# Recurrence preparation traced ahead, fewer vector operations in the projection stage, and a new order of the modulation, in a two-layer diffusion backbone on one core

## The chip, the cores and the metric

The kernel runs on one core of one Trainium2 chip. The core has engines that run side by side, each taking its own instructions in order: TensorE (PE in the profile, with its weight loads as PEld), VectorE (DVE), ScalarE (ACT), GpSimd (POOL) and SyncE (SP), which here only issues DMAs. ACT and POOL issue some DMAs too. Engines wait for each other through semaphores. The metric is the device time of one execution in microseconds (us). Lower is better.

## The reference

Two layers work on 512 latent tokens of width 1024 and, in the first layer, on 256 context tokens with their own conditioning vector. Each sub-layer is norm, modulation, mixer, norm, gate, residual:

```python
def modulate(h, shift, scale):
    return h * (1 + scale) + shift
def ada_mod(cvec, w, b):
    m = jax.nn.silu(cvec) @ w + b          # six vectors of width 1024
...
        ml = ada_mod(c, ada_w[layer], ada_b[layer])
        mc = ada_mod(c_ctx, ada_w[layer], ada_b[layer])
        hl = modulate(rmsnorm(xl, norm_mix_pre[layer]), ml[0], ml[1])
        if layer % 2 == 0:
            yc, yl = mixer_ab(hc, hl, ...)
        else:
            yc, yl = mixer_mlstm(hc, hl, ...)
        xl = xl + ml[2] * rmsnorm(yl, norm_mix_post[layer])
        hl = modulate(rmsnorm(xl, norm_ffn_pre[layer]), ml[3], ml[4])
        xl = xl + ml[5] * rmsnorm(conv_ffn(hl, ...), norm_ffn_post[layer])
```

The mixer of the first layer projects its input to 23 blocks of 128 columns. Eight of them feed a gating part, which for each of 4 groups and each chunk of 128 tokens norms `v`, multiplies it by a 128x128 matrix over the tokens and gates it with `u`. The other 15 feed a recurrence that runs over the tokens in both directions with 8 heads:

```python
    def step(s, inp):
        r_t, w_t, k_t, v_t, kk_t, b_t = inp
        sa = jnp.einsum('bhvk,bhk->bhv', s, kk_t)
        s = s * w_t[:, :, None, :] - sa[..., None] * b_t[:, :, None, :] + v_t[..., None] * k_t[:, :, None, :]
        return s, jnp.einsum('bhvk,bhk->bhv', s, r_t)
```

## The kernel before

Everything is float32. A projection is split in a high and a low part and made of three matmul passes (lines 266 to 268). The first layer's mixer has three stages.

**Lead-in.** The six token tiles are loaded on ACT's queue, normed and transposed (L363) to `xT`, one 128-column tile `kt` of 8 at a time. Meanwhile `ada_gen(0, ...)` (L144) makes shift and scale of the first modulation: 16 loads of 512 KB on SP's queue, row block by row block of `ada_w`, each multiplied by `silu` (L157) into one bank that sums over the row blocks. So no column of the modulation is there before the last row block. Only then `scale_vec` and L374 to L376 make the modulated halves `hT`, and the first two units (named lora) are projected, first all latent, then all context columns.

**Projection stage.** A *unit* is one block of 128 output columns: `load_w` loads 512 KB, ACT makes the high part (L124), POOL the low part (L125), and PE makes 24 latent matmuls (`pl_`) and 24 context matmuls (`pc_`). `kr(ct)` makes the units of k and r for channel tile `ct` (0 to 3, two heads each), `v(ct)` that of v. `sgu(g)` is the gating part of group `g`: two units (`u`, `vg`), then per group of 2 or 4 token tiles transposes (`vt`), a square sum on ACT (L782), two POOL operations for the inverse root (`rstd_from`, L228 and L229), a scaling on DVE (L784), and a matmul (`pz`, L788), tile by tile.

The preparation of the recurrence has three parts for each `ct`. `prep_e` makes decays and keys (matmuls kkn, zw, za, bon, the rest on DVE and ACT). `prep_n` multiplies them in 24 chunks of 64 tokens (`nx`, `ny`, L532 and L533) and copies blocks of the result to `NF` (L538 to L541, on ACT for nx, on DVE for most of ny). `prep_t` inverts 24 triangular matrices a side: DVE transposes `NF` to `Ai` (L552) and `On` (L554), then a recurrence of 31 steps follows, two DVE operations each (L566, L568), which builds `Ti`. Two transposes (`Td` L573, `Tn` L574), copies to `TT` on ACT (L580, L581), and two groups of small matmuls (`w` L588, copied to `Wm` by L591, then `t` L597, copied to `TT` by L600) end it. NF, On and Ti have one buffer each; Ai, Td and Wm share one.

Loops are written as Python generators. `weave` (L302) interleaves several of them in proportion to given lengths, which gives the order in which instructions are traced. A planner then places each instruction: per engine it takes, among those that it believes ready by its own estimates, the one traced earliest. `tc.high_priority(offset=n)` lowers the rank of what is traced inside it by n, as if it had been traced n instructions earlier. Once placed, each engine keeps its order. After `kr(0)`, `prep_e(0)` is woven with `v(0)` and `kr(1)`; then for ct = 0, 1, 2 `prep_t(ct)` is woven with `prep_e(ct+1)` and `prep_n(ct+1)`, and with `v(ct+1)`, `kr(ct+2)` and `NA[ct]` of the 16 parts of the gating.

**Chain stage.** The pools of the stage before are closed, and the recurrence runs over 12 chunks for the pairs of channel tiles (0, 1) and (2, 3), in six blocks `b` of `chains` (L923 on): three per pair. Each block is woven with the loads and matmuls for the next (`preps`), with `prep_t(3)` in block 0 (`inverse`), and with the next two parts of the modulation (`ada_gen(1)`, `ada_gen(2)`, one yield per row block) in blocks 1 and 2. After block 2 `run(ada)` makes their tail, and `gate_rows` and `scale_vec` use them. `finish` of the first pair (means, variances, gate) runs in blocks 3 and 4 with a single PSUM bank, "7".

The output projection, the first feed-forward part and the second layer follow. PSUM has 8 banks, "0" to "7"; `bank(name, role)` takes the banks in the string `role` in turn.

Of the kernel before, what the change touches and what calls it, by code (L numbers as in the profile page):

```python
# [8 lines left out]
F32 = mybir.dt.float32  # L9
F32R = mybir.dt.float32r  # L10
AF = mybir.ActivationFunctionType
ALU = mybir.AluOpType
# [4 lines left out]
KT = 8  # L17
# [57 lines left out]
def _build(ctx, tc, xall, par, cst, ada_w, ada_t, w_in, w_out, ffn_up, ffn_down, lora, wsT, a_bs, c_in, c_gate, c_out, mneg, parf, parm, out):  # L75
# [68 lines left out]
    def ada_gen(g, pool, tag, rawb, cols=1024, rtag="araw", width=None):  # L144
# [5 lines left out]
        for kt in range(KT):  # L150
            for c0 in range(0, n, cols):
                pl = pool[(c0 // cols) % len(pool)] if isinstance(pool, list) else pool
                raw = pl.tile([P, width], F32, tag=rtag, name=f"ada{g}{kt}{c0}", bufs=rawb)[:, :cols]
                nc.sync.dma_start(raw, ada_w[kt, :, g * 2048 + c0:g * 2048 + c0 + cols])
# [175 lines left out]
    with ExitStack() as lx:  # L330
# [10 lines left out]
        with ExitStack() as nx:  # L341
            npool = nx.enter_context(tc.tile_pool(name="nrm0", bufs=1))
            xt = [npool.tile([P, D], F32, tag="xt", name=f"x0_{i}", bufs=6) for i in range(6)]
            for i in (2, 3, 4, 5, 0, 1):
                nc.scalar.dma_start(xt[i], xall[i])
            ag = ada_gen(0, npool, "67", 6)
            silu_rows("67")
            for _ in range(KT):
                next(ag)
            xT = npool.tile([P, KT, T], F32, name="xT0")  # L350
            for (t0, nt, c0) in ((2, 4, 0), (0, 2, TL)):
                dgs = []
# [6 lines left out]
                w = nt * 128  # L359
                for kt in range(KT):  # L360
                    pt = bank(f"nT_00{t0}{kt}", "243501")
                    for i in range(nt):
                        nc.tensor.transpose(pt[:, i * 128:(i + 1) * 128], xt[t0 + i][:, kt * 128:(kt + 1) * 128], ident)  # L363
                    (A.copy if kt % 2 else V.tensor_copy)(xT[:, kt, c0:c0 + w], pt[:, :w])
            run(ag)
            scale_vec(0, 0)
            lw01 = [load_w(w_in[20 + i], f"win{20 + i}") for i in range(2)]
            lps = [[], []]
            for (cnd, c0, w) in ((0, 0, TL), (1, TL, TC)):
                hh, hl = hT[2 * cnd:2 * cnd + 2]  # L370
                for kt in range(KT):
# [5 lines left out]
                for i in range(2):  # L377
                    lps[i].append(proj_pass(lw01[i], hT, f"lora{i}", "0167", cnd))
# [142 lines left out]
        def prep_n(ct):  # L521
# [6 lines left out]
            for g8 in range(3):  # L528
# [6 lines left out]
                for (pp, b0, e) in ((px, 0, A), (py, 64, V)):  # L535
# [11 lines left out]
        def prep_t(ct, prbank):  # L547
# [5 lines left out]
            On = wkT.tile([P, 24, 32], F32, tag="On", name=f"On{ct}")  # L553
            V.transpose(On, NF[:, 1, 0:24])  # L554
# [3 lines left out]
            for s_ in range(31):  # L558
# [199 lines left out]
        def sgu(g):  # L758
# [13 lines left out]
            for (t0, nt) in ((0, 2), (2, 4)):  # L772
# [4 lines left out]
                vns = []  # L777
                for i in range(nt):
                    tk = t0 + i
                    ss = sm.tile([P, 1], F32, tag="ss", name=f"sgss{g}{tk}", bufs=6)  # L780
                    vn = wkR.tile([P, P], F32, tag="vn", name=f"vn{g}{tk}", bufs=5)
                    A.activation(vn, pt[:, i * 128:i * 128 + 128], AF.Square, accum_out=ss)  # L782
                    r = rstd_from(ss, f"sg{g}{tk}", 1.0 / 128)
                    V.tensor_scalar(vn, pt[:, i * 128:i * 128 + 128], r, None, ALU.mult)  # L784
                    vns.append(vn)
                pz = bank(f"pz{g}{t0}", role)
                for i in range(nt):
                    mm(pz[:, i * 128:i * 128 + 128], vns[i], wsT_s[:, g * 128:g * 128 + 128], start=True, stop=True)  # L788
# [138 lines left out]
        for b, (k, g) in enumerate(blocks):  # L927
# [24 lines left out]
            if b == 4:  # L952
# [601 lines left out]
```

## Time and profile before

| | us |
|---|---|
| median of 3 runs | 1988.01 (1987.05 to 1990.56) |
| profiled execution | 1996.04 |
| its span, first to last instruction | 1994.3 |
| PE / DVE / ACT / POOL busy in the span | 1862.3 / 1343.8 / 782.6 / 319.4 |

The page cuts the span in 40 slices of 50 us; each digit is the busy share in tenths. Here are the three rows that matter:

```profile
PE   6998988589997999999999999999999989999998
DVE  3498766783345479999995336676777677777533
...
PEclk8999789698998999999999999999999989999999
```

PEclk is the TensorE clock that was granted. The mixer of the first layer fills the first 13 slices. A group of instructions is named by its line, engine, operation and tiles (written `<-` read); "idle before" is how long the engine stood before them, and what ended that.

### The profile page before, as it was taken

The page shows a single profiled execution, that of the slowest core. Times are in us where ns is not written, and L with a number is a line of the kernel's source. Part 1 is how long each engine was busy: PE and PEld are TensorE (multiplying, and loading weights), DVE is VectorE, ACT ScalarE, POOL GpSimd, SP SyncE. Part 2 cuts the span into 40 slices and gives each one's busy share as a digit, 9 for nine tenths or more (in the row PEclk, how much of TensorE's full clock was granted, in tenths as well). Part 3 has the DMA queues.
Part 4 walks back from the last instruction along what each step waited for, and adds up shares of the span by engine and source line. Part 5 has one row for each costly group of instructions (what it writes and reads, how often), then busy time and mean ns, then how long its engine had stood idle before and what let it go on. Part 6 is the DMA issues. An engine that isn't in the chain of part 4 may idle for free.

```text
span 1994.3 us, 31593 instructions
## 1 busy us (share of the span) xinstructions
PE 1862.3 (93%) x12307; PEld 1502.4 (75%) x12307; DVE 1343.8 (67%) x2635; ACT 782.6 (39%) x1382; POOL 319.4 (16%) x459
## 2 busy tenths in 40 slices
PE   6998988589997999999999999999999989999998
PEld 2876666476675878888888887778888768888886
DVE  3498766783345479999995336676777677777533
ACT  4455545332244442222222225575544343333322
POOL 2222233220100222223221002000110020000001
PEclk8999789698998999999999999999999989999999
DMA  7132121356643424444441324421111312222222
GB/s 289 64 130 104 65 105 43 118 158 197 187 113 138 160 89 157 144 167 167 152 146 62 106 95 150 167 82 42 44 43 43 127 66 95 95 94 90 92 95 85
DMA packets 102694, 227.76 MB, mean 114 GB/s; under 512 B 28160, under 2 KB 42704, under 8 KB 100496
## 3 DMA queue, kind: packets, MB, share of 16 engines
q1 hardware_dynamic: 100192, 219.90, 32.3%
q10 hardware_dynamic: 2192, 5.04, 0.7%
q8 instruction: 97, 1.59, 0.3%
q0 software_dynamic: 160, 0.79, 0.1%
q14 instruction: 53, 0.43, 0.1%
HBM read 199.31 MB, written 26.39 MB: 113 GB/s over the span
## 4 chain that ended last, share of the span: by engine, by line
PE 58%; DVE 2%; ACT 1%; POOL 1%; issue 1%; DMA 0%; DVEq 0%; SPq 0%; POOLq 0%; ACTq 0%
PE of L992 5%; PE of L993 5%; PE of L991 5%; PE pl_fb L268 4%; PE pl_fb L267 4%; PE pl_fa L268 4%; PE pl_fb L266 4%; PE pl_fa L267 4%; PE pl_fa L266 4%; PE pd L1399 1%; PE pe L1376 1%; PE pc_fb L266 1%; PE pc_fa L266 1%; PE pc_fa L267 1%; PE pc_fb L267 1%; PE pc_fb L268 1%
## 5 line engine op out<-in xcount | busy, mean ns | idle before, releaser
L1039 DVE SCALAR_TENSOR_TENSOR cv<-pl_fa,fpar,cv 128x441 f32<-128x441 f32 (+2 forms) x352 | 243.2, 691 | 18.5 <-ACT cv L1028 13.1
L993 PE MATMUL of<-hi_fd,hlo 128*128 128x512 f32 x440 | 173.7, 397 | 3.0 <-DVE hlo L1063 3.0
L992 PE MATMUL of<-lo_fd,hhi 128*128 128x512 f32 x440 | 174.3, 396 | 1.5 <-DVE lo_fd L125 1.5
L991 PE MATMUL of<-hi_fd,hhi 128*128 128x512 f32 x440 | 173.4, 396 | 0.0
L201 DVE SCALAR_TENSOR_TENSOR aj<-am,srb 128x512 f32<-128x512 f32 x224 | 163.7, 731 | 4.8 <-DMA am<-in_ada_t_dram 0.3
L1063 DVE TENSOR_TENSOR hlo<-hid,hhi 128x512 fp32r<-128x512 f32 (+1 forms) x66 | 39.2, 601 | 133.6 <-ACT hhi L1062 133.4
L1062 ACT ACTIVATE hhi<-hid 128x512 fp32r<-128x512 f32 (+1 forms) x66 | 36.7, 558 | 176.4 <-PE of L992 173.0
L993 PEld LDWEIGHTS of<-hi_fd,hlo 128*128 128x128 f32 x440 | 83.4, 190 | 22.5 <-DVE hlo L1063 3.4
L992 PEld LDWEIGHTS of<-lo_fd,hhi 128*128 128x128 f32 x440 | 83.0, 189 | 21.8 <-DVE lo_fd L125 2.7
L222 POOL TENSOR_SCALAR rstd_p_f<-sq_f,sq_f 128x1 f32<-128x1 f32 x10 | 6.8, 680 | 570.3 <-ACT jk_f L970 570.3
L991 PEld LDWEIGHTS of<-hi_fd,hhi 128*128 128x128 f32 x440 | 83.1, 189 | 19.8 <-ACT hi_fd L124 0.4
L125 DVE TENSOR_TENSOR lo_fd<-raw_fd,hi_fd 128x1024 fp32r<-128x1024 f32 x66 | 80.8, 1224 | 25.1 <-ACT hi_fd L124 24.9
L124 ACT ACTIVATE hi_fa<-raw_fa 128x1024 fp32r<-128x1024 f32 x44 | 46.5, 1058 | 92.6 <-PE pl_fb L267 66.7
L124 ACT ACTIVATE hi_fd<-raw_fd 128x1024 fp32r<-128x1024 f32 x66 | 69.2, 1049 | 27.8 <-DMA raw_fd<-in_ffn_down_dram 11.1
L124 ACT ACTIVATE hi_fb<-raw_fb 128x1024 fp32r<-128x1024 f32 x44 | 46.7, 1061 | 74.4 <-PE pc_fa L267 42.9
L125 POOL TENSOR_TENSOR lo_win<-raw_win,hi_win 128x1024 fp32r<-128x1024 f32 x23 | 56.9, 2476 | 92.9 <-ACT hi_win L124 92.8
L268 PE MATMUL pl_fa<-h0f_lathi,lo_fa 128*128 128x512 f32 x176 | 70.3, 399 | 0.0
L268 PE MATMUL pl_fb<-h0f_lathi,lo_fb 128*128 128x512 f32 x176 | 70.3, 399 | 0.0
L268 PE MATMUL pl_fb<-h1f_lathi,lo_fb 128*128 128x512 f32 x176 | 70.2, 399 | 0.0
L268 PE MATMUL pl_fa<-h1f_lathi,lo_fa 128*128 128x512 f32 x176 | 70.2, 399 | 0.0
L1041 ACT ACTIVATE cv<-cv 128x512 f32<-128x512 f32 x44 | 27.8, 632 | 106.4 <-DVE cv L1039 106.4
L125 POOL TENSOR_TENSOR lo_fb<-raw_fb,hi_fb 128x1024 fp32r<-128x1024 f32 x22 | 59.0, 2684 | 65.0 <-ACT hi_fb L124 65.0
(631 smaller groups left out, 5520.2 us busy)
## 6 DMA issues: line engine op xcount, KB each, us to landing
raw_fd<-in_ffn_down_dram SPq DMA_DIRECT2D x66, 512.0 KB, 3.2
am<-in_ada_t_dram SPq DMA_DIRECT2D x112, 256.0 KB, 2.9
raw_fa<-in_ffn_up_dram SPq DMA_DIRECT2D x44, 512.0 KB, 3.3
raw_fb<-in_ffn_up_dram SPq DMA_DIRECT2D x44, 512.0 KB, 3.2
ada<-in_ada_w_dram SPq DMA_DIRECT2D x24, 512.0 KB, 6.4
raw_win<-in_w_in_dram SPq DMA_DIRECT2D x23, 512.0 KB, 3.2
ada<-in_ada_w_dram SPq DMA_DIRECT2D x8, 1024.0 KB, 5.3
raw_cin<-in_c_in_dram SPq DMA_DIRECT2D x16, 512.0 KB, 3.5
```

Source lines behind the costliest of these rows:

```text
L124: nc.scalar.activation(hi[:, c], raw[:, c], AF.Copy)
L125: strm.sub.tensor_tensor(lo[:, c], raw[:, c], hi[:, c].bitcast(F32), ALU.subtract)
L201: V.scalar_tensor_tensor(place(f"aj{i}{h}{cnd}", "junk"), raw, 1.0, sb[cnd * 2 + h], ALU.mult, ALU.mult, accum_out=acc[:, cnd, h:h + 1])
L266: mm(p, wh[:, kt, :], hh[:, kt], start=(kt == 0), stop=False)
L267: mm(p, wh[:, kt, :], hl[:, kt], start=False, stop=False)
L268: mm(p, wl[:, kt, :], hh[:, kt], start=False, stop=(kt == KT - 1))
L991: mm(o[i][hf], hi, w[0][:, c], start=f, stop=False)
L992: mm(o[i][hf], hi, w[1][:, c], start=False, stop=False)
L993: mm(o[i][hf], lo, w[0][:, c], start=False, stop=e)
L1039: V.scalar_tensor_tensor(dv, src[:, r0 + dy:r1 + dy, c0 + dx:c1 + dx], fw(ky * 3 + kx), dv, ALU.mult, ALU.add)
L1062: A.activation(hi, hid[cnd][:, k], AF.Copy)
L1063: V.tensor_tensor(lo, hid[cnd][:, k], hi.bitcast(F32), ALU.subtract)
```

## The change

It has five parts.

1. **Lead-in.** The token tiles are loaded first, half on SP's and half on ACT's queue. The first modulation's weights come packed by output column tile (`ada_0`, 8 loads of 1 MB, three buffers), so that one load gives shift and scale of one `kt`: 8 matmuls of 256 columns, summed over four partition groups by a matmul with `sel`, and `gsc`. For each `kt` follow the transposes, L374 to L376, and the parts of the first two units for that `kt`.
2. **Vector operations.** All NF copies are on ACT. The gating's inverse roots and scaling are made once for each group of 2 or 4 token tiles.
3. **On** is transposed behind the recurrence.
4. **Ahead.** `prep_e`, `prep_n` and `prep_t` (0 to 2) are traced with a rank 200 instructions earlier, and `NA` is (2, 6, 8).
5. **Chain stage.** The next modulation runs in blocks 1 to 4, four row blocks in each, with its tail after block 4. `finish` of the first pair uses banks "01".

```diff
-            for i in (2, 3, 4, 5, 0, 1):
-                nc.scalar.dma_start(xt[i], xall[i])
-            ag = ada_gen(0, npool, "67", 6)
-            silu_rows("67")
-            for _ in range(KT):
-                next(ag)
+            for k, i in enumerate((2, 3, 4, 5, 0, 1)):
+                (nc.sync, nc.scalar)[k % 2].dma_start(xt[i], xall[i])
...
+            def ada_load(c):
+                raws[c] = npool.tile([P, KT, 256], F32, tag="araw", name=f"ada0{c}", bufs=3)
+                nc.sync.dma_start(raws[c].rearrange("p k c -> p (k c)"), ada_0[c])
+            def ada_block(c):
+                raw = raws[c]
+                pb = bank(f"ada0{c}", "2")
+                for k0 in (0, 4):
+                    for q in range(4):
+                        mm(pb[32 * q:32 * q + 32, 0:256], silu[:, k0 + q, :], raw[:, k0 + q], start=not k0, stop=k0 > 0)
+                sb = npool.tile([P, 256], F32, tag="adasb", name=f"adasb0{c}", bufs=2)
+                A.copy(sb, pb[:, 0:256])
+                pt = bank(f"adat0{c}", "3")
+                for k in range(2):
+                    mm(pt[:, 2 * k:2 * k + 2], sb[:, k * 128:k * 128 + 128], sel, start=True, stop=True)
+                o = PC.at["ada_b0"][0] + c
+                V.tensor_tensor(mod[0][:, :, c:c + 9:8], ..., ALU.add)
+                V.tensor_scalar(gsc[(0, 0)][:, :, c], mod[0][:, :, 8 + c], 1.0, pc("mix_pre0", c), ALU.add, ALU.mult)
...
+            for kt in range(KT):
+                if kt + 2 < KT:
+                    ada_load(kt + 2)
+                ada_block(kt)
...
+                    for i in range(2):
+                        wh, wl = (e.rearrange("p (k c) -> p k c", k=KT)[:, kt] for e in lw01[i])
+                        p = lps[i][cnd]
+                        mm(p, wh, hh[:, kt], start=(kt == 0), stop=False)
+                        mm(p, wh, hl[:, kt], start=False, stop=False)
+                        mm(p, wl, hh[:, kt], start=False, stop=(kt == KT - 1))
+            silu_rows("2")
...
-                for (pp, b0, e) in ((px, 0, A), (py, 64, V)):
+                for (pp, b0, e) in ((px, 0, A), (py, 64, A)):
...
-            On = wkT.tile([P, 24, 32], F32, tag="On", name=f"On{ct}")
-            V.transpose(On, NF[:, 1, 0:24])
             Ti = wkT.tile([P, 32, 32], F32, tag="Ti", name=f"Ti{ct}")
...
+            On = wkT.tile([P, 24, 32], F32, tag="On", name=f"On{ct}")
+            V.transpose(On, NF[:, 1, 0:24])
             Td = wkT.tile([P, 32, 32], F32, tag="Ai", name=f"Td{ct}")
...
-                    r = rstd_from(ss, f"sg{g}{tk}", 1.0 / 128)
-                    V.tensor_scalar(vn, pt[:, i * 128:i * 128 + 128], r, None, ALU.mult)
+                G.tensor_scalar(ss[:, :nt], ss[:, :nt], 1.0 / 128, EPS, ALU.mult, ALU.add)
+                G.tensor_tensor(ss[:, :nt], ss[:, :nt], eps_t[:, 2:3].to_broadcast([P, nt]), ALU.pow)
+                V.tensor_tensor(vn[:, :nt * 128].rearrange("p (a q) -> p a q", q=128), pt[:, :nt * 128].rearrange("p (a q) -> p a q", q=128),
+                                ss[:, :nt].unsqueeze(2).to_broadcast([P, nt, 128]), ALU.mult)
...
+        def ahead(gen):
+            while True:
+                with tc.high_priority(offset=AHEAD):
+                    try:
+                        next(gen)
+                    except StopIteration:
+                        return
+                yield
+        AHEAD = 200
-        NA = (4, 6, 6)
+        NA = (2, 6, 8)
         run(kr(0))
-        weave((start_prep(0), 8), (chained(v(0), kr(1), part(0)), 3 + 0))
-        run(prep_n(0))
+        weave((ahead(start_prep(0)), 8), (chained(v(0), kr(1), part(0)), 3 + 0))
+        run(ahead(prep_n(0)))
         for ct in range(3):
             n = NA[ct]
-            weave((prep_t(ct, prbank), 13, 0.0), (chained(start_prep(ct + 1), prep_n(ct + 1)), 9 + 3, 0.0),
+            weave((ahead(prep_t(ct, prbank)), 13, 0.0), (ahead(chained(start_prep(ct + 1), prep_n(ct + 1))), 9 + 3, 0.0),
                   (chained(v(ct + 1), *([kr(ct + 2)] if ct < 2 else []), part(n)), 3 + n, 0.0))
...
-            elif b < 3:
-                todo.append((part_of(ada, 8), 8))
-            elif b == 3:
+            elif b < 5:
+                todo.append((part_of(ada, 4), 4))
+            if b == 3:
                 for ct in range(2):
                     load_bv(ct)
-                F01 = finish((0, 1), ys[0], ("7", "7"))
+                F01 = finish((0, 1), ys[0], ("01", "01"))
...
+            if b == 4:
                 run(ada)
                 gate_rows(0, 0, "7")
                 scale_vec(0, 1)
```

More of the change, by code (lines that the diff above doesn't have):

```diff
@@ L72, in build, with _build @@
         _build(ctx, tc, *args, **kw)
-def _build(ctx, tc, xall, par, cst, ada_w, ada_t, w_in, w_out, ffn_up, ffn_down, lora, wsT, a_bs, c_in, c_gate, c_out, mneg, parf, parm, out):
+def _build(ctx, tc, xall, par, cst, ada_0, ada_w, ada_t, w_in, w_out, ffn_up, ffn_down, lora, wsT, a_bs, c_in, c_gate, c_out, mneg, parf, parm, out):
     nc = tc.nc
@@ L343, in _build @@
             xt = [npool.tile([P, D], F32, tag="xt", name=f"x0_{i}", bufs=6) for i in range(6)]
-            for i in (2, 3, 4, 5, 0, 1):
-                nc.scalar.dma_start(xt[i], xall[i])
-            ag = ada_gen(0, npool, "67", 6)
-            silu_rows("67")
-            for _ in range(KT):
-                next(ag)
+            for k, i in enumerate((2, 3, 4, 5, 0, 1)):
+                (nc.sync, nc.scalar)[k % 2].dma_start(xt[i], xall[i])
+            sel = sm.tile([P, 2], F32, name="sel")
+            V.tensor_tensor(sel, ident[:, 0:2], ident[:, 32:34], ALU.add)
+            for q in (64, 96):
+                V.tensor_tensor(sel, sel, ident[:, q:q + 2], ALU.add)
+            gsc[(0, 0)] = cp.tile([P, 2, 8], F32, name="gsc00")
+            raws = {}
+            def ada_load(c):
[13 more added lines that the diff above has]
+                o = PC.at["ada_b0"][0] + c
+                V.tensor_tensor(mod[0][:, :, c:c + 9:8], pt[:, 0:4].rearrange("p (k r) -> p r k", r=2),
+                                par_s[:, o:o + 9:8].unsqueeze(1).to_broadcast([P, 2, 2]), ALU.add)
+                V.tensor_scalar(gsc[(0, 0)][:, :, c], mod[0][:, :, 8 + c], 1.0, pc("mix_pre0", c), ALU.add, ALU.mult)
             xT = npool.tile([P, KT, T], F32, name="xT0")
             for (t0, nt, c0) in ((2, 4, 0), (0, 2, TL)):
-                dgs = []
                 for i in range(t0, t0 + nt):
@@ L358, in _build @@
                     V.tensor_scalar(xt[i], xt[i], r, None, ALU.mult)
-                w = nt * 128
-                for kt in range(KT):
-                    pt = bank(f"nT_00{t0}{kt}", "243501")
+            for c in range(2):
+                ada_load(c)
+            lw01 = [load_w(w_in[20 + i], f"win{20 + i}") for i in range(2)]
+            lps = [[bank(f"pl_lora{i}", "01"), bank(f"pc_lora{i}", "67")[:, :TC]] for i in range(2)]
+            for kt in range(KT):
+                if kt + 2 < KT:
+                    ada_load(kt + 2)
+                ada_block(kt)
+                for (t0, nt, c0) in ((2, 4, 0), (0, 2, TL)):
+                    w = nt * 128
+                    pt = bank(f"nT_00{t0}{kt}", "45")
                     for i in range(nt):
                         nc.tensor.transpose(pt[:, i * 128:(i + 1) * 128], xt[t0 + i][:, kt * 128:(kt + 1) * 128], ident)
[L364 to L371, printed above, removed]
+                    (V.tensor_copy if c0 else A.copy)(xT[:, kt, c0:c0 + w], pt[:, :w])
+                for (cnd, c0, w) in ((0, 0, TL), (1, TL, TC)):
+                    hh, hl = hT[2 * cnd:2 * cnd + 2]
                     h = xT[:, kt, c0:c0 + w]
@@ L376, in _build @@
                     V.tensor_tensor(hl[:, kt], h, hh[:, kt].bitcast(F32), ALU.subtract)
-                for i in range(2):
-                    lps[i].append(proj_pass(lw01[i], hT, f"lora{i}", "0167", cnd))
+                    for i in range(2):
[5 more added lines that the diff above has]
+            silu_rows("2")
         sx = ExitStack()
```

17 lines of the change are left out of this document (7 added, 10 removed).

## The prediction

> **What bounds the kernel now.** I first read the head of the page, then the table of stretches with four of them, cut where the trace changes its work: the lead-in (norm, first modulation, first two units), the projection stage, the chain stage, and all the rest.
>
> ```profile
> span 1994.3 us, 31593 instructions
> ```
> ```profile
> 0.00:62.00 62.00, 46.64 (x215) 24.46 (x215) 28.07 (x61) 26.54 (x47) 16.33 (x28) 0.92 0.61 241
> 62.00:392.00 330.00, 281.68 (x2135) 227.74 (x2134) 236.41 (x405) 164.53 (x277) 96.04 (x100) 0.88 0.24 89
> 392.00:655.00 263.00, 228.02 (x3509) 172.84 (x3510) 137.28 (x347) 91.41 (x218) 31.13 (x64) 0.90 0.54 163
> 655.00:1994.30 1339.30, 1305.96 (x6451) 1077.38 (x6449) 942.01 (x1824) 500.12 (x841) 175.91 (x268) 0.99 0.31 105
> ```
>
> The columns after the length are busy time of PE, PEld, DVE, ACT and POOL, then granted clock, DMA share and GB/s. The last 1339 us are PE-bound (1306 busy, clock 0.99) and no edit reaches them: they cost after what they cost now. Everything to win or lose lies in the first 655 us, where PE idles and its clock falls to about 0.9. In the projection stage PE idles 330 - 281.7 = 48 us and DVE is busy 72%: neither is full, so a chain that passes between engines sets the pace. The timeline of DVE shows it. Ai (L552) begins the recurrence of a tile `ct`, Td (L573) ends it:
>
> ```profile
> 130.23 1.97 DVE L552 STREAM_TRANSPOSE Ai<-NF 128x1024 f32<-128x1024 f32 x1 [0.29 <-ACT NF L540]
> ...
> 187.51 1.25 DVE L573 STREAM_TRANSPOSE Td<-Ti 128x1024 f32<-128x1024 f32 x1
> ...
> 217.03 2.07 DVE L552 STREAM_TRANSPOSE Ai<-NF 128x1024 f32<-128x1024 f32 x1
> ...
> 275.10 1.25 DVE L573 STREAM_TRANSPOSE Td<-Ti 128x1024 f32<-128x1024 f32 x1
> ...
> 309.96 0.98 DVE L554 STREAM_TRANSPOSE On<-NF 128x768 f32<-128x768 f32 x1 [9.52 <-PE w L588]
> ...
> 313.91 1.95 DVE L552 STREAM_TRANSPOSE Ai<-NF 128x1024 f32<-128x1024 f32 x1
> ...
> 375.75 1.25 DVE L573 STREAM_TRANSPOSE Td<-Ti 128x1024 f32<-128x1024 f32 x1
> ...
> 391.05 1.90 DVE L552 STREAM_TRANSPOSE Ai<-NF 128x1024 f32<-128x1024 f32 x1
> ```
>
> So the stage is: 130.2 us up to the first Ai; three recurrences of 57.3, 58.1 and 61.8; and three turnarounds from Td to the next Ai of 29.5, 38.8 and 15.3. Ai, Td and Wm share one buffer, so a turnaround holds at least Td, the TT copies, both matmul groups (w, t) and their copies. The third shows that this takes no more than 15.3 when little else is in the way. The first two are 14 and 23 us longer.
>
> **The change part by part.** *Vector operations.* The waits of DVE in 62 to 392, then its groups:
>
> ```profile
> DVE vn L784 <- POOL rstd_sg L229: 17.0, 17, 3.1
> ...
> DVE On L554 <- PE w L588: 13.1, 3, 9.5
> ...
> DVE NF L538 <- PE ny L533: 6.1, 6, 2.6
> ```
> ```profile
> L566 DVE TENSOR_TENSOR fs<-Ai,Ti 128x31 f32<-128x31 f32 (+15 forms) x93 | 40.4, 434 | 1.9
> L568 DVE TENSOR_TENSOR Ti<-Ti,fs 128x31 f32<-128x31 f32 (+15 forms) x93 | 35.0, 376 | 2.1
> ...
> L784 DVE TENSOR_SCALAR vn<-vt,rstd_sg 128x128 f32<-128x128 f32 x24 | 8.3, 345 | 18.7 <-POOL rstd_sg L229 17.0 <-ACT hi_win L124 1.7
> L538 DVE COPY NF<-ny 32x512 f32<-32x512 f32 x12 | 8.3, 689 | 6.3 <-PE ny L533 6.1
> ...
> L540 DVE COPY NF<-ny 32x256 f32<-32x256 f32 x12 | 5.2, 430 | 0.2
> L792 DVE SCALAR_TENSOR_TENSOR vg<-pz,par_s,bsb 128x256 f32<-128x256 f32 (+1 forms) x8 | 4.9, 618 | 10.2 <-PE pz L788 10.2
> ```
>
> The NF copies leave DVE: 8.3 + 5.2 = 13.5 busy and 6.1 of waits. The 24 scalings become 8, of the same shapes from PSUM as L792's 8, so about 4.9 instead of 8.3: 3.4 less. Their waits for POOL fall from 17 to about 8 (8 waits of about 1). On behind the recurrence no longer stands at DVE's head waiting for the w matmuls of the tile before: 13.1 less. Together some 45 us of DVE time, but DVE isn't full, so only what lies in the chain counts.
>
> What it costs: the copies go to ACT, at the price of the ones that ACT makes already.
>
> ```profile
> L580 ACT COPY TT<-Td 32x768 f32<-32x768 f32 x6 | 9.2, 1535 | 12.7 <-DVE Td L573 12.7
> ...
> L538 ACT COPY NF<-nx 32x512 f32<-32x512 f32 x12 | 6.8, 569 | 3.2 <-PE nx L532 3.1
> ...
> L540 ACT COPY NF<-nx 32x256 f32<-32x256 f32 x12 | 4.4, 363 | 0.2
> ```
>
> That is 3 x (0.57 + 0.36) = 2.8 more per tile. ACT is busy 50% of the stage, which hides it, except in a turnaround: NF has one buffer, On now reads it behind the recurrence, so the NF copies of tile ct+1 can't start before tile ct's recurrence is over. Then ACT has in one turnaround four TT copies (about 6.1) and all NF copies, and the nx/ny banks, which w and t also use, stay held until these are made. POOL's zeroing of NF and On itself (about 1 us) join that chain.
>
> *Preparation traced ahead.* A priority 200 instructions earlier lets the planner issue kkn, zw, za, nx, w, t and the DVE and ACT work around them before the projection units. In the second turnaround On, at 309.96, has waited 9.5 us for w, which PE had put behind two projection units. With the priority I set the turnarounds to 22, 22 and 19: the 15.3 of the third, about 1 for On, 2.8 of ACT, and 3 for what can't be interleaved, less in the last where only NF(3) comes in. That is -7.5, -16.8 and +3.7, so **-20.6**. The recurrences: 75.4 / 3 = 25.1 us of a window of about 59 is the recurrence itself, the rest is DVE work of the next tile, which stays; the waits and shorter scalings inside give about -3 each, **-10**. Up to the first Ai, two NF groups (2 x 1.12) and the convolutions of kr(1) between them (about 3) go behind: **-6**. The setd writes that are issued ahead wait on SP before w_in loads; those run two buffers early, so I take 0 for them; without that cover, a unit's start would wait for its load.
>
> That is -37, but PE has its own floor: 281.7 busy at clock 0.88 is 248 us of work at full clock, so with the lead-in and one turnaround the stage can't end before 62 + 248 + 15 = 325. Ending at 354 would already need PE 90% full ahead of the last turnaround, so I give 7 back: **-30**, bounds +15 and -66.
>
> *Lead-in.*
>
> ```profile
> 5.00:15.00 10.00, 6.95 (x21) 1.23 (x21) 0.45 (x2) 1.60 (x3) 0.00 (x0) 1.00 1.03 420
> ```
> ```profile
> 28.13 0.87 PE L363 MATMUL nT<-cst_s,x 128*128 128x128 f32 x6
> ...
> 28.94 1.05 PE L157 MATMUL ada<-ada,silu 128*32 128x512 f32 x4
> ...
> 41.52 0.50 PE L266 MATMUL pl_lora<-h_lathi,hi_win 128*128 128x512 f32 x1 [2.24 <-ACT h_lathi L374]
> ...
> 61.41 0.67 PE L472 MATMUL zwb<-twd,lw 64*128 64x256 f32 x2
> ```
> ```profile
> 62.00:82.00 20.00, 5.63 (x24) 4.44 (x24) 1.50 (x2) 0.69 (x1) 1.00 0.22 79
> ```
> ```profile
> 62.00:82.00 20.00, 3.04 (x24) 3.01 (x24) 0.35 (x1) 0.46 (x1) 1.00 0.22 79
> ```
>
> Today the units wait for the whole modulation: they run from 41.5 to 61.4. (The last two rows are one unit's latent and context pass, kT's: 5.63 and 3.04 us.) After, each of 8 column blocks feeds them as it lands. Bytes are the same, and they flow at 420 GB/s with the DMA share at 1.03, so loading ends no earlier. By the Trainium skill, "DMA: Bandwidth & Descriptors", section "Issuing engines are not separate DMA queues", loads issued from two engines share the same 16 engines and save only issue time; the saturated share agrees, and by that rule the split of the x loads is worth 0. The order does help: x ahead of the modulation. PE per block: ada 1.0, transposes 0.9, two units' eighth 2 x 8.67 / 8 = 2.2, sums and waits about 0.7: 4.8, so 8 take 38 us. Started at about 17 that ends at 55 instead of 61: **-6**, bounds -20 (paced by the loads) and +5 (every block pays its ACT-PE-DVE-ACT round trip on PE).
>
> *Chain stage.* PE is nearly full there, so moving half of the modulation matmuls from blocks 1 and 2 to 3 and 4 moves PE time and saves none. What goes are stalls:
>
> ```profile
> 540.00:545.00 5.00, 3.00 (x25) 1.34 (x27) 1.04 (x3) 0.27 (x1) 0.00 (x0) 0.63 0.43 128
> 545.00:550.00 5.00, 5.00 (x44) 3.98 (x41) 1.14 (x7) 1.11 (x3) 0.40 (x1) 0.50 0.01 2
> ```
> ```profile
> 542.00 1.92 PE L157 MATMUL ada<-ada,silu 128*32 128x512 f32 x4 [3.19 <-DMA ada<-in_ada_w_dram]
> ```
> ```profile
> 543.96 0.68 DVE L162 COPY adasb<-ada 64x512 f32<-64x512 f32 x1 [6.70 <-PE ada L157]
> ...
> 548.23 0.28 DVE L327 COPY ggr<-ggt 16x128 f32<-16x128 f32 x1 [0.87 <-PE ggt L325]
> ...
> 551.19 0.42 DVE L738 COPY yc<-cen0b 128x256 f32<-128x256 f32 x1 [2.67 <-PE cen0b L421]
> ```
>
> PE waited 3.2 us for the last load, and then ran at half clock: (0.37 + 0.50) x 5 = 4.3 us of clock. By the Trainium skill, "TensorE: Matmul & The Clock Gate", section "Part 1: The HAM clock gate", a window of about 3.4 us of idling drops the clock to half; the rows agree, and by it the two losses go together. At half the DMA rate both should go: -7.5. `finish` in one bank alternated PE with DVE and ACT (2.7 for one round of four); two banks should halve that, -5, though prep_g uses the same two. Against it the modulation's tail at the end of block 4 (about 4.5, as from 543.96 to 548.5 in these rows, PE taking its part in order): +4.5. **-8**, bounds -18 and +8.
>
> **Sum**: -6 - 30 - 8 = -44 against the profiled execution's 1996.0 (span 1994.3): 1952. The runs' median is 1988.0, 8 less, of the same program; so **1944**, its own range 1925 to 1964.
>
> **The rivals.** *The turnaround stays long* (0.2). NF held by On puts 3 x 0.93 more and all older NF copies on ACT beside the TT copies, and w and t wait for banks. For it: the single buffer. Against it: the third turnaround, 15.3, has most of that and no units. Then turnarounds save nothing, -6 - 4 in the stage, -4 and -6 outside: -20, **1968**. It covers as well a planner that moves little, because data, not rank, held the preparation back.
>
> *PE's floor is reached* (0.18). For it: 62 to 120 is PE-full already, and the units of the gating part are free filler. Stage -55, lead-in -10, chains -13: -78, **1910**.
>
> *Slower: PE stands behind the preparation* (0.1). PE takes its order from the planner. What is ranked ahead has to be issued ahead also where the planner believed its inputs early. Some 13 groups per tile (kkn, zw, za, bon, nx/ny, w, t), 52 in all: above 44 / 52 = 0.85 us of mean wait added per group the gain is gone; at 1.2 it is +18, **2006**. Against it, what such groups wait for now is little:
>
> ```profile
> PE bon1b L421 <- DVE bv L514: 1.8, 1, 1.8
> ...
> PE nx L532 <- ACT NF L541: 1.3, 2, 1.1
> ```
>
> *Nothing visible* (0.05): the parts cancel, within 0.2%, 4 us, about what a measurement of this kernel can tell from no change.
>
> **How the numbers follow.** Forecast 0.47, rivals as above. Above 1982 lie the slower case, the same case and a corner of the first rival, 0.15; below 1907 some 0.07. So the range is 1907 to 1982. Faster by over 0.2% is 0.47 + 0.2 + 0.18 = 0.85, same 0.05, slower 0.10.
>
> **What would show it.** Turnarounds from Td to Ai of about 20 us and a stage end near 355; DVE's waits for rstd_sg and for w gone; PE idle time in the projection stage under 35 us. The first rival shows as ACT NF copies between Td and Ai with turnarounds of 28 and more; the slower case as PE waits over 1 us at kkn, zw, nx, w, t. Wrong would also be any change after the chains. The lead-in step is wrong if zw's first matmul stays at 61; the chain step, if the last block of modulation still ends in a wait for DMA with the clock at 0.5.

## The result: 3.9% slower

| | us |
|---|---|
| before, median of 4 runs | 1988.03 (1987.05 to 1990.56) |
| after, median of 3 runs | 2065.66 (2065.43 to 2065.86) |
| after / before, 95% interval | 1.0393 [1.0378, 1.0407] |
| predicted | 1944 (1907 to 1982) |

One execution of after (7533 us), two of e6 (an experiment below) and one of before in a later series took far longer than the others of the same kernel and are left out. The page of after, the head and the rows that answer to those of before:

```profile
span 2064.1 us, 31747 instructions
## 1 busy us (share of the span) xinstructions
PE 1923.4 (93%) x12399; PEld 1544.0 (75%) x12399; DVE 1322.8 (64%) x2609; ACT 799.8 (39%) x1417; POOL 303.5 (15%) x427
## 2 busy tenths in 40 slices
PE   6886989896999889999999999989999989999998
...
DVE  4375645726334447999999433856777758877534
...
PEclk9997787967999999999999999999999999999999
```

A slice is now 51.6 us. PE looks fuller than before (1923 us against 1862), and yet the kernel is slower. In the ninth slice (413 to 464 us) PE is at 9, its clock at 6 and DVE at 2; from the fourth to the tenth the clock is below 9 in all but one. The extra time is PE time, and it is in the projection stage. Windows of that stage, from the first zwb matmul to the first Qs of the chains, first before, then after with its three turnarounds (columns as in the prediction: length, PE, PEld, DVE, ACT, POOL, clock, DMA share, GB/s):

```profile
61.40:410.50 349.10, 291.67 (x2221) 236.11 (x2222) 252.45 (x436) 167.47 (x283) 108.08 (x118) 0.86 0.26 96
```
```profile
179.00:224.10 45.10, 41.05 (x329) 28.77 (x328) 9.96 (x13) 16.91 (x25) 3.45 (x3) 0.70 0.08 30
...
276.00:334.90 58.90, 53.82 (x375) 34.52 (x376) 13.55 (x20) 24.09 (x37) 5.83 (x4) 0.73 0.10 32
...
396.60:453.30 56.70, 56.70 (x356) 37.14 (x355) 8.19 (x12) 18.50 (x36) 6.75 (x6) 0.70 0.02 8
...
63.50:502.70 439.20, 370.75 (x2234) 271.22 (x2234) 250.69 (x441) 185.76 (x312) 96.07 (x86) 0.79 0.22 76
```

The stage is 90 us longer with nearly the same matmuls (2221 and 2234 records), and 79 of the 90 are PE busy time. Part of that is the lower clock: busy time times clock is 251 us before and 293 after, so by this estimate about 42 us are added work at full clock. In the third turnaround PE is busy all 56.7 us and DVE 8. DVE's timeline says what it stands for there (start, length, in brackets the idle time before and its releaser):

```profile
396.61 1.25 DVE L605 STREAM_TRANSPOSE Td<-Ti 128x1024 f32<-128x1024 f32 x1
...
443.52 0.85 DVE L632 COPY TT<-t 32x256 f32<-32x256 f32 x2 [40.70 <-PE t L629]
...
453.26 2.07 DVE L584 STREAM_TRANSPOSE Ai<-NF 128x1024 f32<-128x1024 f32 x1
```

It waits 40.7 us for `t`. And this is what PE does meanwhile, on PE's timeline of the same kernel:

```profile
425.24 0.42 PE L620 MATMUL w<-TT,On 32*32 32x32 f32 x4
425.58 0.47 PE L565 MATMUL ny<-RB,LB 64*64 64x64 f32 x2
425.99 0.58 PE L266 MATMUL pc_vg<-h_ctxhi,hi_win 128*128 128x256 f32 x1
426.50 0.31 PE L620 MATMUL w<-TT,On 32*32 32x32 f32 x2
426.74 0.47 PE L564 MATMUL nx<-RB,LB 64*64 64x64 f32 x2
427.14 0.31 PE L620 MATMUL w<-TT,On 32*32 32x32 f32 x2
427.38 0.47 PE L565 MATMUL ny<-RB,LB 64*64 64x64 f32 x2
427.78 0.31 PE L620 MATMUL w<-TT,On 32*32 32x32 f32 x2
428.02 0.58 PE L267 MATMUL pc_vg<-h_ctxlo,hi_win 128*128 128x256 f32 x1
```

The groups `w`, `ny`, `nx` and a unit (`pc_vg`) go through PE almost one matmul at a time: 32x32, 64x64, 128x128, 32x32. Each step takes 0.24 to 0.51 us. That is the form of the result: few waits, but PE changing all the time between array shapes. Whether the changes themselves cost time, the experiments have to show.

Times of the stage in all kernels, from the DVE rows of Ai and Td and PE's first zwb. "Shape changes" are pairs of neighbouring matmuls in this stage with a different number of active rows or columns of the array (128x128, 64x64, 32x32 and so on), counted in the trace:

| kernel | time / before | first zwb | recurrences | turnarounds | last Ai to Qs | shape changes |
|---|---|---|---|---|---|---|
| before | 1 | 61.4 | 57.3, 58.1, 61.8 | 29.5, 38.8, 15.3 | 19.5 | 67 |
| after | 1.0393 | 63.6 | 49.6, 51.9, 61.7 | 45.1, 58.9, 56.7 | 49.4 | 347 |
| e1 no rank | 0.9943 | 66.2 | 57.9, 65.5, 56.6 | 15.3, 25.9, 26.6 | 18.7 | 67 |
| e2 rank alone | 1.0547 | 60.5 | 57.3, 68.4, 55.9 | 44.6, 77.4, 32.4 | 55.7 | 356 |
| e3 far rank | 1.0145 | 65.3 | 49.7, 50.2, 55.1 | 25.6, 36.6, 46.0 | 73.1 | 97 |
| e4 vector alone | 0.9933 | 61.6 | 59.7, 57.7, 60.4 | 27.6, 28.5, 14.9 | 18.7 | 69 |
| e6, e12 rank not on PE | 1.0116 | 63.7 | 49.6, 52.2, 51.9 | 38.6, 38.8, 47.8 | 22.0 | 117 |
| e15 far, not prep_n | 1.0119 | 65.5 | 50.6, 58.9, 53.0 | 33.4, 35.7, 47.4 | 21.0 | 91 |
| e10 vector, 96 bytes | 0.9865 | 63.2 | 59.6, 58.9, 58.5 | 27.4, 29.1, 15.0 | 18.6 | 69 |
| e11 as e10, far prep_t | 0.9875 | 63.1 | 57.7, 58.2, 44.8 | 24.3, 31.8, 34.2 | 21.5 | 63 |

### The profile page after: what moved, and what is told of

Its sections match the earlier page's. It is cut to its first block, busy times and chain, and to the rows that moved or that the text cites. A ratio compares the mean times of both kernels' runs of the same rounds, so it can differ in the third digit from the quotient of the medians.

```text
span 2064.1 us, 31747 instructions
## 1 busy us (share of the span) xinstructions
PE 1923.4 (93%) x12399; PEld 1544.0 (75%) x12399; DVE 1322.8 (64%) x2609; ACT 799.8 (39%) x1417; POOL 303.5 (15%) x427
## 4 chain that ended last, share of the span: by engine, by line
PE 55%; DVE 2%; ACT 1%; POOL 1%; issue 0%; DMA 0%; DVEq 0%; SPq 0%; ACTq 0%; POOLq 0%
PE of L1035 5%; PE of L1034 5%; PE of L1033 5%; PE pl_fb L266 4%; PE pl_fb L267 4%; PE pl_fb L268 4%; PE pl_fa L267 4%; PE pl_fa L266 4%; PE pl_fa L268 4%; PE pd L1441 1%; PE pe L1418 1%; PE pc_fb L268 1%; PE pc_fa L268 1%; PE pc_fb L267 1%; PE pc_fa L267 1%; PE pc_fb L266 1%
## 5 line engine op out<-in xcount | busy, mean ns | idle before, releaser
L266 PE MATMUL pl_fa<-h0f_lathi,hi_fa 128*128 128x512 f32 x176 | 69.2, 393 | 0.0
L266 PE MATMUL pl_fb<-h0f_lathi,hi_fb 128*128 128x512 f32 x176 | 69.1, 393 | 0.0
L267 PE MATMUL pl_fb<-h0f_latlo,hi_fb 128*128 128x512 f32 x176 | 69.1, 392 | 0.0
L267 PE MATMUL pl_fa<-h0f_latlo,hi_fa 128*128 128x512 f32 x176 | 69.1, 392 | 0.0
```

The costliest lines, as they stand in the source:

```text
L266: mm(p, wh[:, kt, :], hh[:, kt], start=(kt == 0), stop=False)
L267: mm(p, wh[:, kt, :], hl[:, kt], start=False, stop=False)
```

## The experiments

### Which part it is: e1, e2, e4

**e1** takes the rank out of after and keeps all the rest:

```diff
-                with tc.high_priority(offset=AHEAD):
+                with nullcontext():
```

> After with the earlier rank taken away and all other parts kept. Theory (the rank of 200 makes PE alternate between preparation and unit matmuls): turnarounds fall back to about 30, 40 and 15 to 25 us, start-to-start switches between unit and small matmuls from 163 to about 40, time 1950 to 1985, below the kernel before. Rival 'vector operations' and rival 'lead-in': still above the kernel before, 2020 to 2066. Rival 'gating pushed to the end (2, 6, 8)': the gap from the last Ai to the first chain stays near 49 us, time about 2010.

Measured: 1978.15, ratio 0.9943 [0.9925, 0.9961]. The turnarounds are 15, 26 and 27, and the gap behind the last Ai is 18.7, so it isn't `NA` that pushes the gating to the end. The rank costs 1.0393 - 0.9943 = 4.5%, some 89 us, and all the rest together wins 0.6%, as much as the mere place of the buffers (e5, below).

**e2** is before with nothing but the rank (`ahead` around the three generators, `NA` as it was).

> Before plus the earlier rank of 200 around the three preparation generators, nothing else. Theory (rank overlap): 2050 to 2075, turnarounds of 40 us and more, some 160 switches, clock in the turnarounds 0.70 to 0.75. Rivals 'vector operations' and 'lead-in': 1980 to 1995, the turnarounds as before. Rival 'gating pushed to the end': 2010 to 2030, since the gating parts keep their places (4, 6, 6) here.

Measured: 2099.57, ratio 1.0547 [1.0521, 1.0573], worse than after and beyond the expectation. The rivals "vector operations", "lead-in" and "gating pushed to the end" are out as the cause.

**e4** is before with the vector operations alone (all NF copies on ACT, On traced behind the recurrence, joint gating sums).

> Before plus the vector operations only: all NF copies on ACT, On traced behind the recurrence, the combined gating sums. Theory (rank overlap alone is to blame): 1970 to 1988, a gain of 0 to 18 us, from DVE's lost copies and waits. Rival 'vector operations': 2010 or more, with the turnarounds 10 to 20 us longer because ACT makes the NF copies between the TT copies.

Measured: 1976.16, ratio 0.9933 [0.9915, 0.9952]. The second turnaround falls from 38.8 to 28.5, the other two by 2 or less. ACT's additional copies cost nothing that shows.

### How the rank costs time: e9, e3, e6 and e12, e15, e11

**e9** measures the change of shape by itself. Behind the kernel's output, PE makes 48 unit-sized and 48 small matmuls (or pairs), first in two groups, then in turn. It adds this work and leaves nothing out:

```diff
+        for k in range(NM):
+            big(pu)
+        for k in range(NM):
+            fn(ps, k)
...
+        for k in range(NM):
+            big(pu)
+            fn(ps, k)
```

> Before plus a tail of PE work behind the output: 48 unit-sized matmuls (128x512, float32r) and 48 small ones, first grouped and then alternating one for one, three times: small = pairs of 64x64 float32 (as nx and ny), pairs of 64x64 float32r, single 128x64 float32. Theory (each change between a unit matmul and a small float32 one costs PE by itself, with nothing waited for): grouped about 48 x 0.23 and 48 x 0.07 to 0.12 us, alternating 48 x 0.6 to 0.7, so 0.15 to 0.2 us per change at full clock. Rival (alternation costs nothing in itself, the 163 changes only mark a PE that waits for other engines): alternating equals the sum of the grouped parts within 10%. Which of the three alternations is dear tells whether type or shape makes the price.

Windows of that tail: 64x64 float32 pairs grouped and in turn, then two 64x64 float32r matmuls, both on the first 64 rows, grouped and in turn, then single 128x64 float32 matmuls with all 128 rows and 128 columns of the array grouped and in turn:

```profile
1990.50:2007.30 16.80, 16.80 (x242) 14.55 (x240) 0.00 (x0) 0.00 (x0) 0.00 (x0) 1.00 0.01 2
2007.30:2040.60 33.30, 33.30 (x243) 18.29 (x241) 0.00 (x0) 0.00 (x0) 0.00 (x0) 1.00 0.00 1
2040.60:2059.30 18.70, 18.70 (x145) 16.46 (x145) 0.00 (x0) 0.00 (x0) 0.00 (x0) 0.88 0.00 1
2059.30:2110.90 51.60, 51.60 (x146) 27.53 (x145) 0.00 (x0) 0.00 (x0) 0.00 (x0) 0.50 0.00 0
2110.90:2135.20 24.30, 24.30 (x145) 21.68 (x146) 0.00 (x0) 0.00 (x0) 0.00 (x0) 0.89 0.00 1
2135.20:2157.00 21.80, 21.80 (x145) 19.66 (x144) 0.00 (x0) 0.00 (x0) 0.00 (x0) 1.00 0.00 1
```

The same matmuls with no wait at all take 33.3 instead of 16.8 us when they alternate: 16.5 / 48 = 0.344 us a round, 0.17 for each change of shape, at full clock. With the small ones in the same shape as the unit (last two rows) alternating costs nothing, although the type changes from float32r to float32: 5.5 us of the grouped row ran at half clock, and at full clock it would be about 21.6 us, against 21.8 in turn. So the shape makes the price, not the type. (The float32r pair of rows runs at two clocks and gives no price.) The Trainium skill states such a rule on the page "TensorEngine Tiling (Array Packing)", section "Key Properties": a change of the tiling mode, and not just of the tile, drains the engine. The rows agree, and give the size that the page doesn't.

After has 347 - 67 = 280 more changes than e1: 280 x 0.17 = 48 us at full clock, and the stage's clock is 0.79. That is an estimate: half of after's changes are between 128x128 and 32x32, for which no run has a price.

**e3** puts the rank 4000 instructions ahead, so that the preparation's ranks no longer lie among those of the units and the two are not merged:

```diff
-        AHEAD = 200
+        AHEAD = 4000
```

> After with the rank 4000 instructions earlier instead of 200, so that the ranks of the preparation lie wholly ahead of the units' and no longer among them. Theory (ranks that overlap are merged one for one): switches back to 40 to 60, turnarounds under 30 us, time 1950 to 1990. Rival 'preparation ahead is bad in itself' (the units and the gating slide to the end, PE waits for preparation): 2040 to 2080, no better than after.

Measured: 2019.45, ratio 1.0145 [1.0121, 1.0170]: between the two. The changes are nearly gone (97) and half of the loss with them. The other half stays; now 73 us pass between the last Ai and the first Qs.

**e6** and, for its profile, **e12** keep after's rank of 200 for all but `nx`, `ny`, `w` and `t`:

```diff
-                    mm(px[0:64, ...
+                    with later():
+                        mm(px[0:64, ...
...
+        later = lambda: tc.high_priority(offset=-AHEAD)
```

> After with the earlier rank kept for everything in the preparation except PE's own small matmuls nx, ny, w and t, which keep their place. Theory (PE's alternation one for one between small and unit matmuls is what costs): about 41 switches instead of 164, time 1970 to 1995. Rival 'the rank harms by what it moves on the other engines, or by pushing the units and the gating to the end': 2030 or more.

> The kernel with the rank kept for all but nx, ny, w and t once more, for a profile (its first profile fell into a disturbed run, its timed runs gave 2010 and 2012 us). Theory (what is left, 32 us over the kernel without rank, is PE idling inside the recurrences and turnarounds because DVE and ACT serve the preparation first and the units' banks come free late): PE busy in the projection stage back at 292 to 300 us instead of 371, PE idle 80 us or more instead of 57. Rival (still switching): PE busy 320 or more.

Measured: 2010 and 2012 (ratio 1.0116 [1.0089, 1.0143]), and 2008.5 in e12: between the two expectations of e6. The stage in e1 and in e12:

```profile
66.00:407.20 341.20, 294.55 (x2221) 238.83 (x2222) 245.11 (x396) 179.39 (x307) 95.96 (x86) 0.86 0.28 98
```
```profile
63.00:448.60 385.60, 308.50 (x2221) 246.21 (x2222) 227.93 (x396) 177.67 (x306) 95.30 (x86) 0.83 0.24 87
```

So the alternation on PE is worth 1.0393 - 1.0116 = 2.8%, 55 us. The price gives much the same: 230 fewer changes x 0.17 = 40, divided by the stage's clock of 0.79 some 50. So does busy time times clock, 293 us in after and 256 in e12: 37 at full clock. Why the clock is lower in after wasn't tested. What is left, 1.0116 - 0.9943 = 1.7% or 34 us, is mostly something else: e12 has 50 changes more than e1, by the price about 10 us. PE busy is 308.5 against e1's 294.6, over the 292 to 300 of e12's theory and under the 320 of its rival; idle time is 77 against 47, a little under the 80 expected. The stage is 44 us longer, and 30 of these are idle time. In PE's waits (sum, times, longest) of e12's stage one stands out:

```profile
PE nx L565 <- DVE LB L535: 30.8, 4, 9.9
```

PE stood 30.8 us at `nx`, which keeps its own rank here, for DVE's `LB`. That number fits the 34 us very well, so it became the theory for **e15**: the far rank for `prep_e` and `prep_t`, none for `prep_n`.

```diff
-        AHEAD = 200
+        AHEAD = 4000
...
-            weave(..., (ahead(chained(start_prep(ct + 1), prep_n(ct + 1))), 9 + 3, 0.0),
+            weave(..., (chained(ahead(start_prep(ct + 1)), prep_n(ct + 1)), 9 + 3, 0.0),
```

> After with the rank 4000 earlier for start_prep and prep_t, and prep_n (nx, ny, NF) at its own place. Theory (nx at the head of PE's queue, waiting for LB, is the other 31 us): nx waits for LB under 8 us in sum instead of 25 to 31, time 1970 to 1988. Rival (any preparation ahead pushes the units back): 2000 or more, with turnarounds of 35 us and more.

Measured: 2013.07, ratio 1.0119 [1.0104, 1.0135]. The wait is half (15.8) and the time the same, and but for the first turnaround (33) the rival's numbers came. So the wait at `nx` isn't the price by itself. It isn't shown to be free either: unlike e12, e15 ranks `w` and `t` ahead as well, and PE's waits at `w` and `pz` rose from 8 to 24 us. What e12 and e15 share shows in the sums of the three recurrences, e1 first, then e15, then e12:

```profile
sum 180.00, PE 155.53 PEld 124.42 DVE 165.74 ACT 94.43 POOL 48.87; mean PE 51.84 PEld 41.47 DVE 55.25 ACT 31.48 POOL 16.29
```
```profile
sum 162.50, PE 118.53 PEld 90.36 DVE 145.40 ACT 77.35 POOL 43.71; mean PE 39.51 PEld 30.12 DVE 48.47 ACT 25.78 POOL 14.57
```
```profile
sum 153.70, PE 111.18 PEld 86.18 DVE 143.59 ACT 65.00 POOL 34.50; mean PE 37.06 PEld 28.73 DVE 47.86 ACT 21.67 POOL 11.50
```

In the recurrences DVE is the bound (166 of 180), and PE has its units to make beside it. Ahead, the recurrences get shorter by 18 and 26 us, but PE makes 37 and 44 us less in them: part of the time what stands at its head is preparation that waits for the same DVE. PE's unit work slides into the turnarounds, where DVE has next to nothing to do. In sum over the turnarounds, e1 and then e15:

```profile
sum 67.80, PE 58.22 PEld 49.10 DVE 26.38 ACT 44.29 POOL 12.28; mean PE 19.41 PEld 16.37 DVE 8.79 ACT 14.76 POOL 4.09
```
```profile
sum 116.50, PE 97.48 PEld 78.61 DVE 31.52 ACT 64.54 POOL 20.89; mean PE 32.49 PEld 26.20 DVE 10.51 ACT 21.51 POOL 6.96
```

49 longer there, 18 shorter in the recurrences: 31, which is the 35 us of e15 against e1 but for 4. That it is PE work that slid is shown (37 us less busy in the recurrences, 39 more in the turnarounds); which of the waits at PE's head (`nx`, `bon`, `pz`, each some us) moved how much of it stays open.

**e11** gives the far rank to `prep_t` alone, on the best kernel below.

> The kernel before plus vector operations and 32 bytes, plus a rank 4000 earlier for prep_t alone (recurrence, TT, w, t), while start_prep and prep_n keep their place. If the turnarounds can be shortened by rank without PE standing at nx: turnarounds 15 to 20 us, 1945 to 1960. Rival (any rank ahead delays the units more than it saves): turnarounds shorter but recurrences or the end longer, 1970 or more.

Measured: 1964.96, the same as without (1963.79), and between the two expectations. The third recurrence gets 14 us shorter and the turnaround behind it 19 longer. So even the part that holds the chain from Td to Ai wins nothing by rank. The loss of e15 against e1 would then lie with `prep_e`, which wasn't run by itself.

### The lead-in and the chain stage: e7, e8

**e7** is before with the lead-in alone, **e8** with the chain stage's order alone.

> Before plus the lead-in alone (first modulation in eight column blocks, its units' matmuls between them). Prediction on record: first zwb near 55 instead of 61.4 us. Theory from the runs so far (first zwb at 63.6, 65.3 and 66.2 in the three kernels that have it): first zwb at 63 to 66, so 2 to 5 us lost there. The rest moves by placement alone (32 bytes): time 1980 to 1998.

> Before plus the chain stage's order alone (modulation in blocks 1 to 4, finish in two banks); no buffer moves. Prediction on record: -8 us, time about 1980, from the chain stage (208 us from first to last Qs down to about 200). Rival (it gains nothing when the projection stage isn't late: 209 us in the kernel without the rank, 204 in the kernel with the vector operations alone): 1984 to 1992, chain stage 204 to 210.

e7: 1984.00, ratio 0.9974 [0.9961, 0.9988]. The first zwb starts at 65.3, the first Ai at 138.3, 8 later than before. PE's waits in e7's lead-in:

```profile
PE ada L364 <- DMA ada<-in_ada_dram: 11.2, 2, 10.3
...
PE zwb L504 <- DMA lw<-in_lora_dram: 2.8, 1, 2.8
```

Of the modulation's loads PE waits for those of the first two blocks alone; the third has landed at 22.6 us. Yet PE begins that block only at 28.1, and until then 8 of the 96 matmuls of the two units have run. From 16.7, where the second block begins, to 62.5 PE is busy 42.2 of 45.8 us, and zwb waits 2.8 more for its own weights. Up to about 31 us the matmuls are slow: those of 128x512 start 0.43 us apart at 30 us and 0.24 at 32. That e7 is yet faster than before is none of the lead-in's doing: its buffers move the rest of the kernel by 32 bytes (next part).

e8: 1994.31, ratio 1.0038 [1.0025, 1.0051]: slower, and above both expectations. The chain stage, up to the first output projection, in e8, in a kernel whose instructions stand in before's order (e13, below), and in after:

```profile
406.70:640.40 233.70, 211.97 (x3382) 157.20 (x3382) 112.90 (x305) 81.63 (x202) 19.78 (x46) 0.95 0.49 152
```
```profile
406.50:633.80 227.30, 203.79 (x3382) 153.54 (x3382) 113.35 (x305) 81.98 (x202) 19.73 (x46) 0.95 0.52 157
```
```profile
502.70:727.80 225.10, 207.72 (x3367) 156.78 (x3367) 95.41 (x258) 76.73 (x199) 19.23 (x46) 0.96 0.52 157
```

PE idles 21.7 instead of 23.5 us, so the stalls did shrink; but the same 3382 matmuls take 8 us more. The trace counts 214 changes of shape instead of 184, most of the new ones between 128x128 and 128x64: 30 x 0.17 = 5 of the 8 us, by e9's price. That is an estimate, for e9 never alternates 128x128 with the array shape 128x64, and no run takes these changes away alone. e1, which has this order too, has the same stage (233.8). After's stage is shorter because it begins late, with 18 us of its DVE work done (95.4 instead of 113.4).

### Where the buffers lie: e5, e13, e14, e10

Behind the chains the edits change nothing, and yet the stretch from the first output projection to the end took 1351.4 us in before and 1336.3 in after, with the same 6493 matmuls:

```profile
642.90:1994.30 1351.40, 1318.06 (x6493) 1087.01 (x6493) 949.89 (x1836) 507.26 (x854) 175.91 (x268) 0.99 0.31 106
```
```profile
727.80:2064.10 1336.30, 1300.77 (x6493) 1086.04 (x6493) 947.31 (x1836) 506.42 (x854) 173.35 (x268) 0.99 0.32 108
```

PE is busy 17 us less. What does differ is the place in SBUF: the small new tiles put the feed-forward weights 96 bytes further on (48096 instead of 48000 from the start of a partition). **e5** moves them by as much in before, **e13** and **e14** by 128 and 64 bytes, with an unused tile and no other edit; the engines' order of instructions is that of before:

```diff
+    pad = cp.tile([P, 24], F32, name="pad")
+    nc.gpsimd.memset(pad, 0.0)
```

> Before plus an unused buffer of 96 bytes per partition in front of the small constants, so that every buffer behind it lies 96 bytes further on, as it does in the kernel after; no other edit. Theory (the 15 us that the stages behind the chains lose in after come from where the ffn weights lie in SBUF): the stretch from the first output projection to the end falls from 1351 to about 1336 us, a pl_fa matmul from about 234 to 227 ns start to start; time 1972 to 1982. Rival (the chain order or the lead-in's data layout does it): 1351 as before, time 1986 to 1992.

> Before plus an unused buffer of 128 bytes per partition; the order of the instructions is that of before on every engine. Theory A (the phase within 128 bytes of the ffn weights and what lies with them decides): as before, 1985 to 1992, the stretch behind the first output projection 1346 to 1352. Theory B (the distance of the shift, or leaving the old place at all, decides): 1972 to 1980.

> Before plus an unused buffer of 64 bytes per partition, order of instructions as before. If phase decides and the kernel with the vector operations alone (64 bytes) showed its share: 1978 to 1984, the stretch behind the first output projection near 1344; the vector operations would then be worth only 2 to 8 of the 13 us of their run.

The same stretch in e5 (96 bytes), e13 (128) and e14 (64):

```profile
635.00:1969.40 1334.40, 1300.07 (x6493) 1085.15 (x6493) 947.44 (x1836) 505.98 (x854) 173.93 (x268) 0.99 0.33 108
```
```profile
633.80:1982.80 1349.00, 1316.89 (x6493) 1084.41 (x6493) 949.69 (x1836) 508.77 (x854) 175.15 (x268) 0.99 0.32 107
```
```profile
635.00:1982.20 1347.20, 1311.89 (x6493) 1080.54 (x6493) 949.19 (x1836) 508.65 (x854) 174.41 (x268) 0.99 0.32 107
```

Times: e5 1975.09, ratio 0.9937 [0.9917, 0.9958]; e13 1987.62, 0.9992 [0.9981, 1.0003]; e14 1986.19, 0.9983 [0.9973, 0.9992]. 128 bytes are as none, 96 win 0.6%, 64 win 0.2%, less than e14 expected. Of the two theories the phase stands and the distance falls. e7, at 32 bytes, has 1341.5. Whether the period is 128 or 64 bytes is open: the matmuls of `pl_fa` start 233 ns apart at 0, 64 and 128 bytes, 229 at 32 (e7) and 227 at 96. Why one phase is better than another wasn't tried.

These three also correct the picture of the chain stage. Before's profiled execution had 232.4 us there, and 29.5 in the first turnaround; e13, in the same order and with the same median time, has 227.3 and 26.6. The profiled execution took 8 us more than the median, and these two differences make 8 us.

**e10** is the vector operations at the good phase (e4 with 32 bytes more).

> Before plus the vector operations plus an unused buffer of 32 bytes per partition, which puts the ffn weights 96 bytes behind where before has them (the vector operations alone put them 64 behind). If placement is worth what the 96 byte run showed and the vector operations themselves about 5 us: 1965 to 1972, the stretch behind the first output projection 1334 to 1337. Rival (the two gains are the same one): 1974 to 1978.

Measured: 1963.79, ratio 0.9865 [0.9846, 0.9885], just below the 1965 to 1972 expected. The two gains add up. It beats both kernels, by 1.4% and about 5%.

## Why the prediction was wrong

The parts as steps of one sum, in ratios of their own runs of before: 96 bytes -0.63% (e5), vector operations -0.72% (e10 to e5), lead-in, chain order and `NA` +0.78% (e1 to e10), the rank off PE +1.73% (e6 to e1), the rank on PE's small matmuls +2.77% (after to e6). In us of 1988: -12.5, -14.3, +15.5, +34.4, +55.1, each good to some 6 us by their intervals.

- **"A priority 200 instructions earlier lets the planner issue kkn, zw, za, nx, w, t ... before the projection units" is the step that failed.** A rank 200 earlier doesn't put the preparation ahead. It puts it level with the units traced 200 instructions before, and the planner merged the two by rank, one for one. The turnarounds were to be 22, 22 and 19; they were 45, 59 and 57. The sum used the same PE time per matmul after as before. It had no term for what a change of shape costs (0.17 us each at full clock in e9, 280 more of them), and with the lower clock that came with it it's the largest of all: 55 us.
- **The floor of PE, "325", and the reading that PE idle time can be won.** The floor took 248 us of work as fixed. It was 371 at a clock of 0.79, that is 293 at full clock. In the same cut before has 251. That PE idles under 35 us was to show success; it idled 68, but 79 of the 90 us lost were busy PE.
- **The recurrences, -3 each**: -8, -6 and 0 in after. Right in direction, and worth nothing: with the preparation out of the way they end sooner, but PE has made less beside them (e15, e12).
- **The slower rival, "PE stands behind the preparation", 0.1, 2006.** It comes nearest to the smaller part: e12, with a third of after's changes, took 2008.5 with 30.8 us of waits at `nx` for `LB`. But with half that wait e15 took as long; what both share is the unit work that leaves the recurrences. That 2006 is close to e12's time is luck, and alone it is far from 2066.
- **On, "no longer stands at DVE's head".** It still does. Traced behind the recurrence, it is placed ahead of it all the same (in e10 at 210.7, with Ai at 220.6), for its input is there. DVE's waits in e10 have it in the first place, with 23.2 us instead of 13.1; the second turnaround gained its 10 us nonetheless:

```profile
DVE On L572 <- PE w L590: 23.2, 2, 16.0
```

- **Vector operations**: inside the -30 of the stage they had no number of their own. Measured -10 (e4 against e14, both at 64 bytes) to -14. ACT's 2.8 us a tile doesn't show, not even in the turnarounds, where the prediction had charged it.
- **SP's queue, taken as 0**: right. In after's projection stage one unit waits for its weights (their high part, on ACT), 1.0 us.
- **Lead-in, -6, was +4 up to zwb and +8 up to the first Ai** (e7). The term that was mis-sized is the work of 38 us from 17 on, 4.8 a block: it took 45.8, and PE was busy 42.2 of them. The 4.8 came from matmuls of before that ran at full speed; e7's ran slower up to about 31 us. "Wrong if zw's first matmul stays at 61" came true: 65.
- **Chain stage, -8.** After shows 200.6 us from the first Qs to the last against 208.1, and one would call that right. It's wrong: alone, the new order makes the stage 6 us longer. The waits for DMA went, as the prediction read them, but the same matmuls took 8 us more of PE, which more changes of shape explain in part (an estimate). The 208.1 belongs to that one execution; e13, in the same order, has 203.0, waits 2.7 us for these loads and shows no half clock there.
- **"They cost after what they cost now"**, of the 1339 us behind the chains: off by 15, for a side effect of the diff, the place of the buffers (e5).

The range left out the time because every case in it let PE's work cost the same.

## What to carry to other kernels

An earlier rank that is smaller than the stretch of work it is to overtake doesn't reorder but interleaves: look at the order it gives on PE, and count neighbours of different array shape, before counting on it. Where one engine bounds a stretch and another fills it, moving the filler's competitors forward can just move the filler to where nothing runs beside it. And before a gain of less than 1% is put down to an edit, run the unedited kernel with its buffers moved by the same number of bytes.

## What was not expected of the hardware

- A change of array shape between neighbouring matmuls cost 0.17 us at full clock, as much as three quarters of a 128x512 matmul (0.227 us start to start), without any wait, and the profile counts it as busy PE.
- In e9 PE was busy in every microsecond of 2059.3 to 2110.9, alternating, at a granted clock of 0.50. A PE that is full on the page can be at half clock. The Trainium skill, "TensorE: Matmul & The Clock Gate", section "Part 1: The HAM clock gate", has the clock fall after a window of idling; no idle time shows here. Alternation alone isn't the reason: the clock had fallen at 2055.0, among the grouped 64x64 float32r matmuls, and the float32 pairs alternated for 33.3 us at 1.00. What brought it down stays open.
- The place of buffers within 128 bytes moved matmul time: 1318 us at 0 bytes, 1317 at 128, 1312 at 64, 1300 at 96, for the same 6493 matmuls at clock 0.99.
